# Large projections first, and the second half's norm inside the first half's projections

## The chip, the cores and the metric

The kernel runs on one core of a Trainium2 chip. The metric is the device time of one execution in microseconds, lower is better. A core has five engines with instruction queues of their own: TensorE (PE, with its weight loads shown as PEld), VectorE (DVE), ScalarE (ACT), GpSimd (POOL) and SyncE (SP), which here issues all DMA transfers of the program.

## What is computed

One step of a decoder trunk with two layers, for 1024 prompt tokens and 64 sample tokens (8 sequences of 8), with D = 1024. Layer 0 mixes with RWKV-7, layer 1 with sparse attention; both end with a feed-forward block. The change lies in layer 0, ahead of the recurrence:

```python
h = rms_norm(x, norm_g) * (1 + sc_a) + sh_a            # sh_a, sc_a, ... = SiLU(c) @ W_ada + b_ada
h_prev = concat([shift_prev, h[:, :-1]])
xr, xw, xk, xv, xa, xg = [h + (h_prev - h) * mix[n] for n in range(6)]
r, k, v = xr @ w_rkv[0], xk @ w_rkv[1], xv @ w_rkv[2]  # 1024 x 1024 each
w = tanh(xw @ w1) @ w2                                 # rank 64
a = sigmoid(a0 + (xa @ a1) @ a2)                       # rank 64
g = sigmoid(xg @ g1) @ g2                              # rank 160
S, y = wkv7_scan(S0, r, decay(w), k, v, a)             # over time, per head
out = (norm(y) + bonus) * g @ w_o
```

All six results are needed by the recurrence, g only at its end. They don't depend on each other.

## The kernel before

**Halves.** The 1088 tokens are worked on in two groups: GA holds the 64 sample tokens and prompt rows 0 to 511 (576 columns, in blocks of 320 and 256), GB the prompt rows 512 to 1023 (one block of 512). Activations lie transposed, features on partitions, as four tiles of [128, 2, 585] ("quarters"). The pool `xp` has four such tiles, enough for one group's x or h. `rwkv_h` writes h over x, and needs for GB the last column of GA's h (`lastA`).

**Projections.** `rwkv_proj(g, h)` is a generator. For each of the six inputs, `mixed` (L526) makes xn = h*(1-mix) + h_prev*mix in eight chunks and splits it into a rounded part and a remainder (hi, lo), and `mm3` (L133, matmuls in L140) multiplies in three terms: hi*wh, lo*wh, hi*wl. A large projection has 8 output blocks of 8 chunks; a low-rank one has a first matmul to the rank, an activation and a split, and a second one to 1024. Before, the three low-rank inputs (n = 1, 4, 5) come first and the three large ones (n = 0, 2, 3) after. All results go to a scratch tensor in DRAM (RA, RB; L591 and L600). The mixed inputs live in `act` (8 tiles, one set of hi and lo). During GA a second set, `act2`, and a pool `mx` for the temporaries exist, and the sets take turns; during GB there is one set.

**Conditioning.** `ada_steps` multiplies SiLU(c) with W_ada, 48 steps that each load 1 MB (L261) and take 16 matmuls (L264) and a fold (L250). Eight steps come before everything else. The other 40 are the generator `more`, stepped once at each of the 36 yields of GA's `rwkv_proj`; the rest runs behind it.

**Recurrence.** `wkv` runs 18 units of GA (16 prompt, 2 sample) and 16 of GB through four stages (prep, inv1, inv2, rec) that are interleaved. Its constants (L181, c_gmask and others) and tiles come from pools opened after those of the conditioning are closed, in the same memory. Each unit reads its columns of RA or RB (L672, and g in L813) and stores its result (YA or YB, L960). `projB()` is handed to `wkv` as `self.side`. The rate for GA's units is 0, so nothing of it is put between them by hand; at t == len(A), ahead of the stages of the last three GA units and of the first GB unit, the loop `for _ in self.side: pass` emits all of it. After that `first(GA)`, the output projection and feed-forward of GA, becomes the side work.

**Order.** A list scheduler turns the program into one fixed order per engine: where an instruction's inputs and tile slots are free, it may go ahead of earlier ones that are not ready, and of several that are ready the earlier one in the program goes first. So what stands later in the program fills idle time, as far as its tiles are free. On the chip each engine, SP too, takes its instructions in that order and waits where a semaphore isn't set yet.

Of the kernel before, what the change touches and what calls it, by code (L numbers as in the profile page):

```python
# [47 lines left out]
GA = Grp("A", 64, 0, 512)  # L48
GB = Grp("B", 0, 512, 512)
# [28 lines left out]
class Kern:  # L78
# [202 lines left out]
    def xtile(self, name, pool=None):  # L281
        return [(pool or self.xp).tile([128, 2, 585], F32, name=name, tag="x") for _ in range(4)]

    def load_x(self, g):
        nc = self.nc
        x = self.xtile("x")
        for c0, n, kind, r0 in g.tiles:
            src = self.I["x_sample"].rearrange("b t d -> (b t) d") if kind == "s" else self.I["x_prompt"][0, r0:r0 + 128]
            for hf in range(2):
                t = self.tmp("xin")  # L290
                nc.sync.dma_start(t[0:n, 0:512], src[:, hf * 512:hf * 512 + 512])
                o = self.mmt()
                for k in range(4):
                    nc.tensor.transpose(o[:, k * 128:k * 128 + n], t[0:n, k * 128:k * 128 + 128], self.ident[0:n, 0:n])
                ov = o.rearrange("p (q a b) -> p q a b", q=2, a=2)
                for q in range(2):
                    (nc.scalar.copy if q else nc.vector.tensor_copy)(x[hf * 2 + q][:, :, c0:c0 + n], ov[:, q, :, 0:n])
        return x
# [253 lines left out]
    def rwkv_proj(self, g, h):  # L552
        nc, W, I = self.nc, g.W, self.I
        R = self.rscr(g)
        self.kn[g.name] = self.cp.tile([128, len(g.tiles), 16], F32, name="kn" + g.name)

        for n, w1, w2, rk, slot in ((1, "rw_w1", "rw_w2", 64, 2), (4, "rw_a1", "rw_a2", 64, 3), (5, "rw_g1", "rw_g2", 160, 5)):
            xs = self.mixed(g, h, n)
            parts = [(0, min(rk, 128))] + ([(128, rk - 128)] if rk > 128 else [])
            mids = []  # L560
            for f0, fn in parts:
                hw, lw = self.loadw(I[w1][0, :, f0:f0 + fn].rearrange("(k p) f -> p k f", p=128), 128, 8 * fn)
                t = self.tmp("lt")

                def evac(o, c0, c1):
                    if n == 4:
                        nc.scalar.copy(t[0:fn, c0:c1], o[0:fn, 0:c1 - c0])
                    else:
                        nc.scalar.activation(out=t[0:fn, c0:c1], in_=o[0:fn, 0:c1 - c0], func=AF.Tanh, scale=(1.0 if n == 1 else 0.5))
                self.mm3(g, [(hw[:, k * fn:k * fn + fn], lw[:, k * fn:k * fn + fn]) for k in range(8)], xs, evac, M=fn)  # L570
                if n == 5:
                    nc.vector.tensor_scalar(out=t[0:fn, 0:W], in0=t[0:fn, 0:W], scalar1=0.5, scalar2=0.5, op0=ALU.mult, op1=ALU.add)
                a, b = self.tmp("lh", F32R), self.tmp("ll", F32R)
                self.split(t[0:fn, 0:W], a[0:fn, 0:W], b[0:fn, 0:W])
                mids.append((a[0:fn, 0:W], b[0:fn, 0:W]))
            ws = [self.loadw(I[w2][0, f0:f0 + fn, :], fn, 1024) for f0, fn in parts]
            for m in range(8):
                t = self.tmp("pt")

                def evac(o, c0, c1):  # L580
                    if n == 5:
                        nc.scalar.copy(t[:, c0:c1], o[:, 0:c1 - c0])
                    else:
                        i0 = (0 if n == 1 else 8) + m
                        nc.scalar.activation(out=t[:, c0:c1], in_=o[:, 0:c1 - c0], func=AF.Tanh, scale=0.5, bias=self.w0h[:, i0:i0 + 1])
                if m % 2:
                    yield
                self.mm3(g, [(hw[0:fn, m * 128:m * 128 + 128], lw[0:fn, m * 128:m * 128 + 128]) for (hw, lw), (_, fn) in zip(ws, parts)], mids, evac)
                if n != 5:
                    nc.vector.tensor_scalar(out=t[:, 0:W], in0=t[:, 0:W], scalar1=0.5, scalar2=0.5, op0=ALU.mult, op1=ALU.add)  # L590
                nc.sync.dma_start(R[m, :, slot, 0:W], t[:, 0:W])  # L591
        for n, i, slot in ((0, 0, 0), (2, 1, 1), (3, 2, 4)):
            xs = self.mixed(g, h, n)
            for m in range(8):
                yield
                hw, lw = self.loadw(I["rw_w_rkv"][0, i, :, m * 128:m * 128 + 128].rearrange("(k p) f -> p k f", p=128), 128, 1024)
                t = self.tmp("pt")
                self.mm3(g, [(hw[:, k * 128:k * 128 + 128], lw[:, k * 128:k * 128 + 128]) for k in range(8)], xs,
                         lambda o, c0, c1: nc.scalar.copy(t[:, c0:c1], o[:, 0:c1 - c0]))
                nc.sync.dma_start(R[m, :, slot, 0:W], t[:, 0:W])  # L600
                if i == 1:

                    if m == 0:
                        ss = self.kn[g.name]
                        if g.ns:
                            nc.vector.memset(ss[:, 0], 1.0)
                    sq = self.tmp("ks")
                    nc.scalar.activation(out=sq[:, 0:W], in_=t[:, 0:W], func=AF.Square, scale=self.rv["kk"][:, m:m + 1])
                    o = self.mmt()
                    for it, (c0, n_, _, _) in enumerate(g.tiles):  # L610
                        nc.tensor.matmul(o[0:n_, it * 2:it * 2 + 2], sq[:, c0:c0 + n_], self.hsel, start=True, stop=True)
                    nt = len(g.tiles)
                    for i0, i1, P in ((0, 1, 64), (1, nt, 128)) if g.ns else ((0, nt, 128),):
                        nc.vector.tensor_scalar(out=ss[0:P, i0:i1, m * 2:m * 2 + 2], in0=o[0:P, i0 * 2:i1 * 2].rearrange("p (i h) -> p i h", h=2),
                                                scalar1=1e-24, scalar2=None, op0=ALU.max)
                    if m == 7:
                        sv = ss.rearrange("p i h -> p (i h)")
                        y = self.rsqrt(None, sv, 128, nt * 16, "kn")
                        nc.vector.tensor_copy(sv, y)
# [934 lines left out]
            nc.sync.dma_start(self.scr["OA"][:, :, 0:64].rearrange("k p t -> p k t"), oTs)  # L1554

    def run(self):
        self.mark("setup" )
        self.setup()
        self.mark("ada_prep" )
# [23 lines left out]
        with ExitStack() as ctx:  # L1583
# [5 lines left out]
            more = more()  # L1589
            act, self.act2 = self.act, P("act2", 8)  # L1590
            self.mx = P("mx", 6)
            for _ in self.rwkv_proj(GA, hA):
                next(more, None)
            self.act = act
            self.act2 = self.mx = None
            for _ in more:
# [13 lines left out]
                pass  # L1610

        def projB():
            self.mark("load_xB")
            x = self.load_x(GB)
            self.mark("spill_xB")
            self.spill_x(GB, x)
            self.mark("rwkv_hB")
            h = self.rwkv_h(GB, x)
            self.mark("rwkv_projB")
            yield from self.rwkv_proj(GB, h)  # L1620

# [130 lines left out]
```

## Time and profile before

| | us |
|---|---|
| median of 3 runs | 4313.54 (4303.31 to 4316.45) |
| the profiled execution | 4326.98 |
| its span | 4325.0 |

The profile shows one execution. The page gives busy time per engine and, in 40 slices of the span, the TensorE clock that the chip granted in tenths of full speed (PEclk). The views used below are the table of windows (busy time of each engine in chosen stretches, with the granted clock and the DMA share), the groups of instructions by source line, the waits, and the timeline. In a group's row, "x400 | 27.8, 391" means 400 instructions, 27.8 us busy in all, 391 ns each, then the idle time of the engine before them and what ended it. Matmuls overlap in the pipeline, so the mean duration of one is longer than the distance from one to the next; where a count of matmuls is priced, busy time in a stretch divided by the count is used.

### The profile page before, as it was taken

The page shows a single profiled execution, that of the slowest core. Times are in us where ns is not written, and L with a number is a line of the kernel's source. Part 1 is how long each engine was busy: PE and PEld are TensorE (multiplying, and loading weights), DVE is VectorE, ACT ScalarE, POOL GpSimd, SP SyncE. Part 2 cuts the span into 40 slices and gives each one's busy share as a digit, 9 for nine tenths or more (in the row PEclk, how much of TensorE's full clock was granted, in tenths as well). Part 3 has the DMA queues.
Part 4 walks back from the last instruction along what each step waited for, and adds up shares of the span by engine and source line. Part 5 has one row for each costly group of instructions (what it writes and reads, how often), then busy time and mean ns, then how long its engine had stood idle before and what let it go on. Part 6 is the DMA issues. An engine that isn't in the chain of part 4 may idle for free. (4 is left out here: it accounts for less than half of the span.)

```text
span 4325.0 us, 77351 instructions
## 1 busy us (share of the span) xinstructions
PE 3993.6 (92%) x31120; PEld 3206.4 (74%) x31120; DVE 2521.2 (58%) x6174; ACT 1681.0 (39%) x3147; POOL 969.0 (22%) x762
## 2 busy tenths in 40 slices
PE   7998899989999999989799979988879999999999
PEld 4787665666777799989655656778666677998887
DVE  5512784533667655551886954452899855555444
ACT  5632564434445323331454323332443344333332
POOL 1321331312333222211111122222110000222322
PEclk6798697978899899989799989998888899999999
DMA  6676122314221122233332245444211112233332
GB/s 215 199 237 207 50 85 69 89 54 124 85 64 54 42 70 85 84 106 117 121 95 63 64 156 202 139 124 153 75 51 35 30 50 79 80 92 93 93 94 88
DMA packets 506743, 433.89 MB, mean 100 GB/s; under 512 B 93777, under 2 KB 451777, under 8 KB 501202
## 3 DMA queue, kind: packets, MB, share of 16 engines
q1 hardware_dynamic: 500498, 391.20, 29.9%
q0 software_dynamic: 5888, 37.75, 2.5%
q8 instruction: 245, 4.01, 0.4%
q14 instruction: 112, 0.92, 0.1%
HBM read 360.48 MB, written 67.87 MB: 99 GB/s over the span
## 5 line engine op out<-in xcount | busy, mean ns | idle before, releaser
L126 POOL TENSOR_TENSOR wl<-w,wh 128x1024 fp32r<-128x1024 f32 (+1 forms) x258 | 618.6, 2402 | 2326.5 <-ACT wh L122 2095.5
L140 PE MATMUL o<-hi,wh 128*128 128x512 f32 (+4 forms) x2592 | 884.1, 345 | 28.5 <-ACT hi L144 24.1
L140 PE MATMUL o<-lo,wh 128*128 128x512 f32 (+4 forms) x2592 | 885.9, 343 | 14.4 <-DVE lo L145 10.9
L140 PE MATMUL o<-hi,wl 128*128 128x512 f32 (+4 forms) x2592 | 881.7, 341 | 4.2 <-DVE wl L126 4.0
L122 ACT CAST wh<-w 128x1024 fp32r<-128x1024 f32 (+3 forms) x388 | 396.1, 1033 | 1010.6 <-PE o L140 829.9
L397 DVE SCALAR_TENSOR_TENSOR xr<-o,mods,xr 128x256 f32<-128x256 f32 (+1 forms) x816 | 463.0, 570 | 298.2 <-PE o L140 286.0
L140 PEld LDWEIGHTS o<-hi,wh 128*128 128x128 f32 (+1 forms) x2592 | 499.0, 194 | 80.7 <-ACT hi L144 28.0
L140 PE MATMUL o<-uh,wh 128*128 128x320 f32 (+2 forms) x1536 | 520.7, 339 | 39.8 <-DVE xr L397 31.8
L140 PEld LDWEIGHTS o<-lo,wh 128*128 128x128 f32 (+1 forms) x2592 | 499.6, 193 | 66.3 <-DVE lo L145 14.3
L140 PEld LDWEIGHTS o<-hi,wl 128*128 128x128 f32 (+1 forms) x2592 | 498.7, 193 | 53.7 <-issue 11.3
L140 PE MATMUL o<-uh,wl 128*128 128x320 f32 (+2 forms) x1536 | 514.2, 336 | 5.5 <-DVE tno L1220 3.7
L140 PE MATMUL o<-ul,wh 128*128 128x320 f32 (+2 forms) x1536 | 512.6, 334 | 0.0
L140 PEld LDWEIGHTS o<-uh,wh 128*128 128x128 f32 x1536 | 293.3, 191 | 77.9 <-DVE xr L397 37.5
L140 PEld LDWEIGHTS o<-uh,wl 128*128 128x128 f32 x1536 | 292.9, 191 | 33.6 <-issue 5.2
L126 DVE TENSOR_TENSOR wl<-w,wh 128x1024 fp32r<-128x1024 f32 (+2 forms) x130 | 184.9, 1423 | 223.3 <-ACT wh L122 222.9
L140 PEld LDWEIGHTS o<-ul,wh 128*128 128x128 f32 x1536 | 293.6, 191 | 25.5 <-issue 3.6
L145 DVE TENSOR_TENSOR ul<-z,uh 128x512 fp32r<-128x512 f32 (+1 forms) x128 | 124.7, 974 | 171.3 <-ACT uh L144 170.5
L1041 PE MATMUL o<-wl,hi 128*128 128x256 f32 (+2 forms) x648 | 189.6, 294 | 6.9 <-POOL wl L126 6.9
L1041 PE MATMUL o<-wh,hi 128*128 128x256 f32 (+2 forms) x648 | 188.7, 293 | 6.9 <-ACT hi L144 6.9
L1041 PE MATMUL o<-wh,lo 128*128 128x256 f32 (+2 forms) x648 | 185.0, 292 | 0.0
L1210 DVE TENSOR_SCALAR_CACHE_REDUCE tj<-sc,tcf 128x384 bf16<-128x384 f32 (+2 forms) x192 | 180.4, 939 | 2.4
L1282 ACT ACTIVATE sm<-sm,st 128x128 f32<-128x128 f32 (+7 forms) x128 | 99.3, 776 | 155.2 <-DVE st L1281 107.7
(415 smaller groups left out, 6902.0 us busy)
## 6 DMA issues: line engine op xcount, KB each, us to landing
w<-in_w_up SPq DMA_DIRECT2D x128, 512.0 KB
w<-in_w_down SPq DMA_DIRECT2D x128, 512.0 KB
wa<-in_w_ada SPq DMA_DIRECT2D x96, 512.0 KB
w<-in_rw_w_rkv SPq DMA_DIRECT2D x48, 512.0 KB
w<-in_att_w_in SPq DMA_DIRECT2D x32, 512.0 KB
RA<-pt SPq DMA_DIRECT2D x48, 288.0 KB
RB<-pt SPq DMA_DIRECT2D x48, 256.0 KB
in<-RA SPq DMA_DIRECT2D x32, 320.0 KB
```

Source lines behind the costliest of these rows:

```text
L122: nc.scalar.copy(h[:kp, :n], w[:kp, :n])
L126: eng.tensor_tensor(out=l[:kp, :n], in0=w[:kp, :n], in1=h[:kp, :n], op=ALU.subtract)
L140: nc.tensor.matmul(o[0:M, 0:c1 - c0], a, b[:, c0:c1], start=(i == 0 and q == 0), stop=(i == n - 1 and q == 2))
L145: (lo_eng or self.nc.vector).tensor_tensor(out=lo, in0=src, in1=hi, op=ALU.subtract)
L397: nc.vector.scalar_tensor_tensor(out=xm[:, p0:c1], in0=o[:, p0 - c0:c1 - c0], scalar=self.mods[l][:, j * 8 + m, 8:9], in1=xm[:, p0:c1], op ...
L1041: nc.tensor.matmul(o[0:n, 0:cw], a, w, start=(k == 0 and q == 0), stop=(k == 7 and q == 2))
L1210: nc.vector.tensor_scalar(out=junk[:, 0:L], in0=s, scalar1=th if isinstance(th, float) else th[:, i:i + 1], scalar2=None, op0=op, op1=ALU. ...
L1282: nc.scalar.activation(out=sm[:, 0:L], in_=sm[:, 0:L], func=AF.Exp, scale=-1.0, bias=mn[:, 0:1], accum_out=sums)
```

## The change

1. `rwkv_proj` is cut in two. The large projections become a generator `proj_rkv` of their own, which `rwkv_proj` runs first, for both halves; the low-rank ones follow.
2. GB's x is loaded, spilled and normed not at the start of `projB`, but inside GA's projections: when the ninth yield is reached (i == 8, at the first output block of the second large projection). Its four tiles come from a new pool `xpB` that is open during GA's projections. The resulting h is stored to a DRAM scratch `hB`.
3. `projB` loads h from `hB` into tiles of `xp` and goes straight to the projections.

The conditioning's generator is stepped as before, once at each of the 36 yields.

```diff
-    def load_x(self, g):
-        nc = self.nc
-        x = self.xtile("x")
+    def load_x(self, g, pool=None):
+        nc = self.nc
+        x = self.xtile("x", pool)
...
         self.kn[g.name] = self.cp.tile([128, len(g.tiles), 16], F32, name="kn" + g.name)
+        yield from self.proj_rkv(g, h)
 
         for n, w1, w2, rk, slot in ((1, "rw_w1", "rw_w2", 64, 2), (4, "rw_a1", "rw_a2", 64, 3), (5, "rw_g1", "rw_g2", 160, 5)):
...
                 nc.sync.dma_start(R[m, :, slot, 0:W], t[:, 0:W])
+
+    def proj_rkv(self, g, h):
+        nc, W, I = self.nc, g.W, self.I
+        R = self.rscr(g)
         for n, i, slot in ((0, 0, 0), (2, 1, 1), (3, 2, 4)):
...
             self.mx = P("mx", 6)
-            for _ in self.rwkv_proj(GA, hA):
+            xpB = P("xpB", 4)
+            for i, _ in enumerate(self.rwkv_proj(GA, hA)):
                 next(more, None)
+                if i == 8:
+
+                    xB = self.load_x(GB, xpB)
+                    self.spill_x(GB, xB)
+                    hB = self.rwkv_h(GB, xB)
+                    self.scratch("hB", [8, 128, 513])
+                    for q in range(4):
+                        nc.sync.dma_start(self.scr["hB"][q * 2:q * 2 + 2].rearrange("k p n -> p k n"), hB[q][:, :, 0:513])
...
         def projB():
-            self.mark("load_xB")
-            x = self.load_x(GB)
-            self.mark("spill_xB")
-            self.spill_x(GB, x)
-            self.mark("rwkv_hB")
-            h = self.rwkv_h(GB, x)
+            h = self.xtile("hr")
+            for q in range(4):
+                nc.sync.dma_start(h[q][:, :, 0:513], self.scr["hB"][q * 2:q * 2 + 2].rearrange("k p n -> p k n"))
             self.mark("rwkv_projB")
             yield from self.rwkv_proj(GB, h)
```

## The prediction

> **What bounds the kernel now.** I read the page first, for the engine that is full and for its clock.
>
> ```profile
> span 4325.0 us, 77351 instructions
> PE 3993.6 (92%) x31120; PEld 3206.4 (74%) x31120; DVE 2521.2 (58%) x6174; ACT 1681.0 (39%) x3147; POOL 969.0 (22%) x762
> PEclk6798697978899899989799989998888899999999
> ```
>
> PE is busy for 92% of the span, but in the first third its granted clock is low. So only two things can save time: stretches in which PE has no work, and stretches in which it works at half clock. The edited code runs in the first 1146 us, which I cut into stages with the table of windows (columns: stretch and length; busy time of PE, PEld, DVE, ACT, POOL; clock; DMA share; GB/s).
>
> ```profile
> 57.00:184.00 127.00, 114.67 (x606) 83.07 (x606) 77.59 (x128) 82.10 (x151) 40.25 (x23) 0.66 0.56 181
> 163.00:184.00 21.00, 21.00 (x88) 14.05 (x88) 4.01 (x9) 9.22 (x18) 5.18 (x3) 0.50 0.36 118
> 184.00:392.00 208.00, 206.12 (x1727) 186.10 (x1727) 45.54 (x96) 72.11 (x136) 49.91 (x25) 0.99 0.73 230
> 392.00:410.00 18.00, 13.30 (x105) 6.80 (x104) 3.25 (x11) 3.29 (x9) 0.74 (x1) 0.67 0.82 267
> 410.00:460.00 50.00, 32.45 (x285) 24.98 (x282) 37.23 (x98) 24.34 (x52) 14.27 (x26) 0.57 0.31 90
> 460.00:665.00 205.00, 190.27 (x2719) 133.39 (x2716) 158.28 (x462) 117.75 (x274) 73.23 (x101) 0.87 0.23 67
> 1040.00:1083.00 43.00, 42.83 (x202) 35.14 (x200) 12.56 (x20) 18.29 (x28) 13.13 (x7) 1.00 0.66 201
> ```
>
> 57 to 184 is the low-rank part of the first half (A), 184 to 392 its three large projections: PE full, clock 0.99. 392 to 410 are leftover steps of the conditioning (w_ada); 410 to 460 load and norm the second half (B) beside the first recurrence units, with PE at 32 of 50 us and clock 0.57. From 460 B's projections fill PE between the units of A. 1040 to 1083 is the other end of that filling, and four rows of SP's timeline show what it is.
>
> ```profile
> 644.50 0.37 SPq L960 DMA_DIRECT2D YA<-gt  x1
> 665.52 0.37 SPq L960 DMA_DIRECT2D YA<-gt  x1
> 1020.18 0.37 SPq L960 DMA_DIRECT2D YA<-gt  x1
> 1083.38 0.33 SPq L600 DMA_DIRECT2D RB<-pt  x1
> 1099.44 0.36 SPq L960 DMA_DIRECT2D YA<-gt  x1
> ```
>
> Each YA store ends a unit of A. Normally they are 21 us apart (644.50, 665.52); here 79 us pass. In program order all that is left of projB stands ahead of the last three A units (the loop that empties `self.side` at t == len(A)). PE does nothing else for 43 us, while the recurrence waits.
>
> ```profile
> 341.00:392.00 51.00, 45.61 (x340) 44.87 (x339) 1.00 0.62 195
> 460.00:1040.00 580.00, 217.59 (x584) 110.87 (x585) 0.82 0.25 71
> 1040.00:1083.00 43.00, 42.01 (x186) 34.39 (x184) 1.00 0.66 201
> ```
>
> These are the same windows for line 140 alone, the projection matmuls. At full clock one takes 45.61/340 = 0.134 us in A (two column blocks, 320 and 256) and 42.01/186 = 0.226 us in B (512 columns). The 43 us are a whole large projection: 8 x 24 x 0.226 = 43.4. B's 768 matmuls (576 large, 192 low-rank) would need 174 us; they take 217.6 + 42.0 = 260. So 86 us go to half clock and to matmuls stretched between others.
>
> **Part 1: large ahead of low-rank in A.** Rows of the groups, 184 to 392:
>
> ```profile
> L264 PE MATMUL oa<-wa,cst 128*32 128x256 f32 x400 | 27.8, 391 | 1.0 <-DMA wa<-in_w_ada 1.0
> L250 PE MATMUL pa<-fold,adas 128*128 128x10 f32 x95 | 14.5, 262 | 0.7 <-ACT adas L266 0.5
> L611 PE MATMUL o<-hsel,ks 128*128 128x2 f32 (+1 forms) x80 | 10.1, 244 | 0.2
> L539 DVE SCALAR_TENSOR_TENSOR xn<-x,vec,mt 128x512 f32<-128x512 f32 x13 | 13.0, 1000 | 0.0
> L537 DVE SCALAR_TENSOR_TENSOR xn<-x,vec,mt 128x64 f32<-128x64 f32 x13 | 5.9, 454 | 3.4 <-ACT mt L532 3.2
> L145 DVE TENSOR_TENSOR lo<-xn,hi 128x576 fp32r<-128x576 f32 x7 | 9.1, 1294 | 5.5 <-PE o L140 4.7 <-ACT hi L144 0.8
> 60.02 0.74 PE L140 MATMUL o<-hi,wh 128*64 128x320 f32 x2 [2.95 <-ACT hi L144]
> 182.39 0.41 PE L140 MATMUL o<-ll,wh 32*128 32x256 f32 x1
> ```
>
> The large part costs 24 x 48 x 0.134 = 154 us, 24 conditioning steps at (27.8 + 14.5)/25 = 1.7 us = 41, key norms 10: 205 of the 208 us seen. It is bound by PE and its order doesn't change that. The low-rank part needs 384 x 0.134 = 51 and 12 x 1.7 = 20, so 71 of its 127 us: the rest is the opening wait for `mixed` and half clock. One `mixed` is eight chunks of 1.0 + 0.45 + half of 1.29 = 2.1 us on DVE, 17 us. Some such wait stays at 60 us whichever projection is first: two of the eight output blocks (2 x 48 x 0.134 = 13 us) fit in it, so I charge 5. The low-rank inputs are then mixed under the third large projection (two sets of `act` tiles), which takes 17 off. Net -12, between -25 and +5. What I keep is the half clock: between 163 and 184 PE is busy for 21.00 of 21 us and still granted 0.50, on matmuls of which half, like the one at 182.39, use 32 rows.
> The Trainium skill, page "TensorE: Matmul & The Clock Gate", section "Part 1: The HAM clock gate", says the opposite: sustained matmuls open the gate within about 3.4 us and only an idle window closes it. The row above speaks against it; by the page the low-rank part would run near its full-clock time, which is the fourth rival below.
>
> **Part 2: B's load and norm inside A.** Groups between 385 and 460:
>
> ```profile
> L368 ACT ACTIVATE x<-hu,mods,gm 128x512 f32<-128x512 f32 x8 | 6.5, 810 | 3.0 <-DVE hu L359 3.0
> L294 PE MATMUL o<-c_ident,xin 128*128 128x128 f32 x32 | 5.7, 334 | 0.0
> L333 DVE TENSOR_TENSOR acc<-acc,sq 128x512 f32<-128x512 f32 x7 | 5.5, 786 | 0.9 <-ACT sq L331 0.8
> L359 DVE TENSOR_TENSOR hu<-x,rb 128x512 f32<-128x512 f32 x8 | 5.5, 682 | 1.5 <-ACT rb L352 1.5
> L297 DVE COPY x<-o 128x256 f32<-128x256 f32 x8 | 3.4, 426 | 2.5 <-PE o L294 2.4
> L351 PE MATMUL o<-c_ident,rsBy 128*128 128x128 f32 x8 | 1.9, 421 | 0.0
> L338 PE MATMUL o<-onec,acc 128*128 128x2 f32 x8 | 1.9, 356 | 1.7 <-DVE acc L333 1.7
> ```
>
> PE gets 5.7 + 1.9 + 1.9 = 9.5 us more in A. That can be 0 if the transposes slip into the opening, which needs only the new pool; 17 if PE, in order, also waits for the sums (a chain of adds and Newton steps). I take 9.5. DVE's 3.4 + 5.5 + 5.5 = 14.4 us lie under the large projections, where DVE is busy 46 of 208. Leaving 410 to 460, the same 14.4 no longer stand between the first units' instructions: -7, half of it, between -14 and 0.
> New on SP: four stores of hB and four loads, 0.53 MB each; 4.2 MB at 230 GB/s are 18 us of transfer, in stretches with a DMA share of 0.73 or less. The eight loads of x and four spills only move. A store of hB waits for L368, and behind it stand weight loads that PE needs; SP mostly waits anyway:
>
> ```profile
> SPq L261 <- PE oa L264: 106.3, 32, 7.1
> ```
>
> so I charge 0, at most 8. The loads of hB wait until A's last `mixed` has read hA; behind them on SP stand the last stores of A and the units' loads, which no engine needs before the conditioning ends. `first(GA)`'s reload of x waits in the same way for B's last `mixed`, as before.
>
> **Part 3: what the end of A releases.** The recurrence's constants are the first thing after the conditioning, in memory that its tiles held:
>
> ```profile
> 410.11 0.33 SPq L181 DMA_DIRECT2D c_gmask<-in_c_gmask  x1
> 457.74 0.73 ACT L532 ACTIVATE mt<-x,mix 128x513 f32<-128x513 f32 x1
> ```
>
> Five conditioning steps are left over after 36 yields; behind a PE that is full they can't start early, and from 392 they are paced by their loads. Behind the low-rank part, where PE is idle 12 of 127 us and at half clock, I expect most to slip in: -12, between -18 and 0.
> B's first `mixed` starts at 457.74 now. Afterwards it needs only hB and A's first `act` set, both free before A's last low-rank outputs, so B's large projections can fill PE from about 390. Supply: PE's idle time between 392 and 460 is 4.7 + 17.6 = 22 us, the 9.5 us are gone from there, and of the 86 us lost in B's matmuls dense early filling should recover some 12. Together 43.5, against the 43.4 that stand at 1040. What may remain is a piece of the last low-rank projection. The gap of 79 less 21 is 58 us; I take 45 of it, between 0 and 58.
>
> **Sum.** -12 + 9.5 - 7 - 12 - 45 = -66.5 us. Against the profiled execution (4326.98 us, span 4325.0) that is 4260.5. This execution lay 13.4 us above the median of the three runs, 4313.54, so in the runs I expect 4247.
>
> **Rivals.**
> 1. *The surplus is not usable*: no change. Units run at 21 us with DVE busy 158 of 205 us, so more filling on PE delays them as much as it advances B, a low-rank projection stands at 1040 instead of a large one, and the conditioning still ends last. Only part 2's 7 us are left: 4306. Against it: the idle 22 us.
> 2. *The low-rank work is exposed at both ends*: slower. In A nothing hides it (no -12, +5, B's PE work with its waits +17). At t == len(A) the last low-rank projection of B and half of another are open: in A the last one took 126 to 184, 58 us, so about 64 instead of 43. 5 + 17 + 21 = +43, 4357. It decides once more than one low-rank projection of B is open when unit 18 starts. For it: DVE's load in 460 to 665, which slows every `mixed`. Against it: B starts 70 us earlier.
> 3. *The norm doesn't move where it says*: nothing but the new pool holds back the loads of x, so they may run in the opening, beside the w_ada loads. 2 MB at 230 GB/s delay those by up to 9 us: 4256, within the forecast's own range.
> 4. *Full clock in the low-rank part*: 127 - 71 = 56 us are lost now, of which I have already taken 17; the other 39 would go too: 4208. Against it: the 163 to 184 row.
>
> **How the numbers follow.** Forecast (with rival 3) 0.66, rival 4 0.07, rival 1 0.14, rival 2 0.13. Its own range is 4210 to 4295 (parts 2 and 3 at their best give -102, 4212; with their savings halved and their costs at the upper ends, -19, 4295). Chances: a measurement of this kernel tells about 0.3%, 13 us, from no change. Faster by more: 0.66 + 0.07 + a quarter of rival 1 = 0.77; within: 0.10; slower: 0.13. For 8 in 10 the range runs from 4195, which takes in rival 4, to 4312, which takes in rival 1 and leaves out rival 2 and the outer ends.
>
> **What would show it.** Right: large stores (RA) from about 75 to 290 us and low-rank ones last; constants issued before 400; B's first `mixed` before 400; YA stores near 1020 without a gap of 79. Wrong in part 1: the low-rank part over 120 us, or under 90 (rival 4). Wrong in part 3: constants still after 405, or a pure block of B's matmuls of 30 us or more ahead of the last A units. The forecast fails as a whole if that block remains, for it carries 45 of the 66 us.

## The result and the profile after

The changed kernel is slower: 4351.16 us in the median of 20 runs (4337.28 to 4372.57), against 4314.99 for 20 runs of the kernel before. The ratio is 1.0106, with a 95% interval of 1.0083 to 1.0128. By the ratio 46 us are lost, by the medians 36, where 66.5 were to be gained. Runs of one kernel differ mostly by the mean clock that they were granted: the changed kernel took 4372.35 us at 0.910 and 4337.28 at 0.920. The loss is not such a difference, for at 0.917 the changed kernel took 4343.95 to 4350.04 us, and the kernel before 4311.09 and 4317.08 (two of its runs beside e13 to e16). The profiled execution took 4343.95 us at 0.917, the one of the kernel before 4326.98 at 0.911. The two traces thus lie only 17 us apart, where the medians lie 36 apart.

The page of the changed kernel, engine totals and clock (tenths of full speed, 40 slices):

```profile
span 4342.2 us, 77414 instructions
PE 3983.3 (92%) x31120; PEld 3190.3 (73%) x31120; DVE 2534.5 (58%) x6174; ACT 1683.1 (39%) x3147; POOL 964.9 (22%) x762
PEclk7896798888898999999799989998888899999999
```

The same number of matmuls keeps PE busy for about as long (3993.6 before). So PE's work hasn't grown; it stands in other places. The table of windows of the changed kernel, cut at its own stages (columns as in the prediction):

```profile
57.00:135.00 78.00, 71.61 (x552) 63.01 (x548) 48.40 (x64) 46.35 (x78) 34.34 (x17) 0.91 0.76 237
135.00:180.00 45.00, 24.91 (x180) 18.63 (x181) 24.27 (x68) 23.78 (x44) 5.28 (x4) 0.77 0.84 240
180.00:309.00 129.00, 127.62 (x1013) 119.74 (x1014) 30.28 (x66) 45.11 (x83) 29.92 (x15) 0.96 0.56 178
309.00:431.00 122.00, 114.27 (x616) 83.30 (x615) 39.18 (x65) 50.17 (x101) 19.21 (x12) 0.67 0.51 165
431.00:455.00 24.00, 15.14 (x100) 6.62 (x100) 1.34 (x8) 1.84 (x6) 0.00 (x0) 0.50 0.77 240
1017.00:1112.00 95.00, 78.03 (x358) 45.24 (x356) 58.43 (x109) 59.57 (x104) 16.83 (x14) 0.76 0.42 139
```

57 to 309 are now A's large projections: 252 us where they took 208. 309 to 431 are the low-rank ones, 122 for 127, still at clock 0.67. 431 to 455 is the conditioning's rest, 24 for 18, at half clock. The sum is 398 for 353: the recurrence's constants come 45 us later.

Most of the 44 us in the large part, some 35, stand in one row of that table, 135 to 180: the load and norm of B. (The other 9 are the opening, as e8 shows below.) SP's timeline brackets the row by the stores of two neighbouring output blocks of A; the two rows behind them show the distance of the next ones:

```profile
130.54 0.33 SPq L605 DMA_DIRECT2D RA<-pt  x1
175.51 0.49 SPq L605 DMA_DIRECT2D RA<-pt  x1
191.35 0.34 SPq L605 DMA_DIRECT2D RA<-pt  x1
201.29 0.34 SPq L605 DMA_DIRECT2D RA<-pt  x1
```

One output takes 45 us where the next ones take 16 and 10. What PE waited for between 130 and 180 (view of the waits: total us, times, longest) names the norm's own chain, link by link, and the conditioning held up beside it:

```profile
PE oa L264 <- DMA wa<-in_w_ada: 6.1, 4, 2.3
PE pa L250 <- ACT adas L266: 4.2, 1, 4.2
PE o L351 <- DVE rsBy L173: 3.5, 1, 3.5
PE o L294 <- ACT x L297: 2.8, 1, 2.8
PE o L338 <- DVE acc L333: 2.5, 1, 2.5
PE o L519 <- DVE lastB L508: 2.5, 1, 2.5
```

The second place is where B's projections start. SP's timeline around the constants; then ACT's row of A's last `mixed`, ACT's row of B's first one, and PE's first matmul of B; then the two largest of SP's own waits between 340 and 460:

```profile
454.75 0.35 SPq L181 DMA_DIRECT2D c_gmask<-in_c_gmask  x1
...
457.05 1.38 SPq L818 DMA_DIRECT2D gt<-RA  x3
458.47 2.04 SPq L1630 DMA_DIRECT2D hr<-hB  x4
```

```profile
347.91 0.79 ACT L532 ACTIVATE mt<-x,mix 128x585 f32<-128x585 f32 x1
462.25 0.72 ACT L532 ACTIVATE mt<-hr,mix 128x513 f32<-128x513 f32 x1 [2.10 <-DMA hr<-hB]
480.18 0.80 PE L140 MATMUL o<-hi,wh 128*128 128x512 f32 x1
```

```profile
SPq L261 <- PE oa L264: 33.6, 18, 6.1
SPq L592 <- ACT pt L583: 32.9, 8, 6.4
```

ACT begins its last reading of A's rows at 347.91 (DVE at 350.13), so their place is free soon after; hB has been in DRAM since about 170. Yet the four loads go out at 458.47, behind all loads of the conditioning and behind the constants, in a queue that spent 66 us of that stretch waiting for the conditioning's matmuls and for A's last outputs. B's first `mixed` waits for them. It comes at 462.25, not before 400 as forecast, and 4.5 us later than before the change. PE's first matmul of B comes at 480.18; before the change it came at 462.07.

The third place is the other end. The last stores of A's units and of B's outputs, changed kernel:

```profile
1003.22 0.37 SPq L965 DMA_DIRECT2D YA<-gt  x1
...
1016.81 0.32 SPq L605 DMA_DIRECT2D RB<-pt  x1
1035.82 9.06 SPq L592 DMA_DIRECT2D RB<-pt  x8
1061.06 8.04 SPq L592 DMA_DIRECT2D RB<-pt  x8
1094.16 14.63 SPq L592 DMA_DIRECT2D RB<-pt  x7
1111.63 0.32 SPq L592 DMA_DIRECT2D RB<-pt  x1
1117.84 0.37 SPq L965 DMA_DIRECT2D YA<-gt  x1
```

The gap between the 15th and 16th YA store was 79 us and is 115: all three low-rank projections of B (L592) stand in it, 95 us in the window 1017 to 1112. In between the units ran faster: from the first YA store (505.46 before, 541.42 after) to the 15th it took 515 us and takes 462. So the lead of the kernel before is 45 us at the constants, 36 at the first YA store, -17 at the 15th, 18 at the 16th and 24 at the last one (1145.01 and 1169.02).

### The profile page after: what moved, and what is told of

Its sections match the earlier page's. It is cut to its first block, busy times and chain, and to the rows that moved or that the text cites. A ratio compares the mean times of both kernels' runs of the same rounds, so it can differ in the third digit from the quotient of the medians.

```text
span 4342.2 us, 77414 instructions
## 1 busy us (share of the span) xinstructions
PE 3983.3 (92%) x31120; PEld 3190.3 (73%) x31120; DVE 2534.5 (58%) x6174; ACT 1683.1 (39%) x3147; POOL 964.9 (22%) x762
## 5 line engine op out<-in xcount | busy, mean ns | idle before, releaser
L126 POOL TENSOR_TENSOR wl<-w,wh 128x1024 fp32r<-128x1024 f32 (+2 forms) x258 | 618.8, 2403 | 2320.1 <-ACT wh L122 2155.5
L140 PE MATMUL o<-hi,wh 128*128 128x512 f32 (+3 forms) x2592 | 887.8, 346 | 24.9 <-ACT hi L144 20.5
L140 PE MATMUL o<-lo,wh 128*128 128x512 f32 (+3 forms) x2592 | 886.6, 343 | 12.7 <-DVE lo L145 11.4
L140 PE MATMUL o<-hi,wl 128*128 128x512 f32 (+3 forms) x2592 | 881.7, 341 | 1.9 <-DVE tno L1225 0.9
L122 ACT CAST wh<-w 128x1024 fp32r<-128x1024 f32 (+2 forms) x388 | 396.0, 1033 | 962.7 <-PE o L140 791.5
L126 DVE TENSOR_TENSOR wl<-w,wh 128x1024 fp32r<-128x1024 f32 (+3 forms) x130 | 183.8, 1414 | 214.7 <-ACT wh L122 214.1
```

The lines of the kernel that those rows point to most:

```text
L122: nc.scalar.copy(h[:kp, :n], w[:kp, :n])
L126: eng.tensor_tensor(out=l[:kp, :n], in0=w[:kp, :n], in1=h[:kp, :n], op=ALU.subtract)
L140: nc.tensor.matmul(o[0:M, 0:c1 - c0], a, b[:, c0:c1], start=(i == 0 and q == 0), stop=(i == n - 1 and q == 2))
```

## The experiments

Each kernel was timed beside the kernel before, in five rounds, 6 to 12 runs of each. Kernels that were not timed side by side are compared by their ratios to it; 0.01 of a ratio is 43 us. "The barrier" is the point where all that is left of B's projections stands ahead of A's last three units. In the expectations, N, O, T1 to T5, A and W are names of theories, explained where they first stand.

Three parts were changed: A's order, B's order, and the place of B's norm. The kernel before, the changed one and six of the runs are their eight combinations. The table shows the ratio to before, the times of the constants' load, of the first and 15th YA store and of the last one, the gap behind the 15th, and how many of B's 48 output blocks were stored ahead of the 15th.

```
kernel   A's order   B's order   B's norm  ratio [95% interval]      const   1st YA  15th YA  gap    last YA  outputs
before   low-rank    low-rank    in projB  1                         410.11  505.46  1020.18   79.3  1145.01  38
e8       large       low-rank    in projB  1.0028 [1.0004, 1.0052]   420.02  505.53  1015.94   83.6  1159.62  37
e7       low-rank    large       in projB  0.9997 [0.9972, 1.0021]   412.44  502.95   987.54  117.0  1154.72  20
e1       large       large       in projB  1.0073 [1.0043, 1.0103]   420.20  510.56  1005.68  119.0  1174.86  20
e2       low-rank    low-rank    in A      0.9963 [0.9934, 0.9992]   439.06  529.75  1028.49   54.8  1125.89  41
e3       large       low-rank    in A      1.0028 [0.9998, 1.0058]   455.82  540.45  1025.77   60.8  1130.50  40
e9       low-rank    large       in A      0.9900 [0.9866, 0.9933]   434.50  517.00  1004.52   70.8  1117.21  32
changed  large       large       in A      1.0106 [1.0083, 1.0128]   454.75  541.42  1003.22  114.6  1169.02  21
```

**First round: the block in A, or the barrier?** The trace left two theories. T1: the loss is the 45 us block of the norm. T2: it is the three low-rank projections at the barrier.

e1: the order alone.

```diff
-                if i == 8:
-                    xB = self.load_x(GB, xpB)
...
         def projB():
-            h = self.xtile("hr")
+            x = self.load_x(GB)
+            self.spill_x(GB, x)
+            h = self.rwkv_h(GB, x)
```

> The order alone: large projections first in both halves, the second half loaded and normed behind the first half's projections, as before the change. Theory T1 (the 45 us by which the recurrence's constants come later are the load and norm of the second half, which stand in TensorE's order ahead of the second large projection: 45 us for one output block in place of some 9): without them the constants are issued at 410 to 425 us (410.11 before, 454.75 after), and the kernel takes about as long as before, 4305 to 4330. Rival T2 (the loss is at the barrier, where three low-rank projections of the second half, 95 us, stand in place of one large one, 43 us): the constants come early as well, but the YA stores keep a gap of 110 to 120 us ahead of the last two, and the time is 4340 or more.

Constants at 420.20, as T1 said, but 4343.17 us and a gap of 119.0, as T2 said.

e2: the norm alone. `yield from self.proj_rkv(g, h)` goes back behind the low-rank loop, and the norm to the first block of the second large projection.

```diff
-                if i == 8:
+                if i == 20:
```

> The norm alone: low-rank projections first in both halves as before, the second half loaded, normed and stored behind the first output block of the second large projection, the same place in the work as in the changed kernel. T1: the output block beside the norm takes 40 to 50 us again, the constants come at 440 to 455, and the time is 4335 to 4355. T2: the gap of the YA stores falls to 45 to 80 us, and the time is 4315 or less, late constants or not.

4300.09 us, faster than before (0.9963), although the constants come at 439.06: the block is there as in the changed kernel, and pays for itself. T1 as the whole cause falls.

e3: the changed kernel with B's order undone.

```diff
-        yield from self.proj_rkv(g, h)
+        if g.ns:
+            yield from self.proj_rkv(g, h)
...
+        if not g.ns:
+            yield from self.proj_rkv(g, h)
```

> As the changed kernel, but the second half does its low-rank projections first, as before the change; the first half is as in the changed kernel. T1: the constants stay at 450 to 460 and the time at 4335 to 4355, since what is done late at the barrier is only what was not done earlier. T2: the gap of the YA stores falls from 115 to 45 to 80 us and the time by 25 to 45, to 4305 to 4325.

4316.70 us, gap 60.8: as T2 said. 0.78 points of ratio come back.

e4: the changed kernel with the norm behind A's projections in the program.

```diff
-                if i == 8:
-                    xB = self.load_x(GB, xpB)
...
+            xB = self.load_x(GB, xpB)
+            self.spill_x(GB, xB)
+            hB = self.rwkv_h(GB, xB)
```

> As the changed kernel, but the second half's load, norm and stores come behind all projections of the first half in the program, ahead of the rest of the conditioning. T1: large outputs run without the 45 us block, the constants come at 410 to 425 if the norm runs beside the conditioning's rest, at 440 to 460 if it runs ahead of it; the time follows them, 4315 to 4330 or 4345 to 4360. T2: the gap of the YA stores stays at 105 to 120 and the time within 10 us of the changed kernel's 4351, wherever the norm runs.

Constants at 445.55, 4334.72 us (1.0042, from 1.0015 to 1.0068), a gap of 114.8. The constants are where T1 has 4345 to 4360 and the gap where T2 has 4341 to 4361; the time is below both.

**Second round: each part alone.** If T2 were the cause, turning round B's order alone should cost what the order costs.

e5 and e6: the norm alone once more, beside the third low-rank projection of A (`i == 9` in place of 20), and behind all of A's projections.

> Low-rank projections first in both halves, and the second half's load and norm in the low-rank part of the first half (beside the third low-rank projection, where TensorE is granted half clock) in place of beside the second large one. Theory N (beside a large projection the norm costs TensorE some 30 us of waiting, because its chain stands in TensorE's order; the low-rank part waits anyway): the constants come at 415 to 430 us (439.06 with the norm beside the large one, 410.11 before), the gap of the YA stores stays at 50 to 70, and the time is 4270 to 4292. Rival O (the chain costs its waits wherever it stands): the constants at 435 to 450 and the time at 4295 to 4310.

> Low-rank projections first in both halves, and the second half's load, norm and stores behind all projections of the first half in the program, ahead of the conditioning's rest. With large projections first this place put the constants at 445.55, 25 us later than without any norm there. N: the chain stands alone there, beside nothing but the conditioning's rest, so the constants come at 425 to 440 and the time is 4295 to 4315. O: the same constants; the two differ in the run with the norm in the low-rank part.

Constants at 433.20 and 429.04, 4304.25 us (0.9968) and 4297.99 (0.994, from 0.9909 to 0.9971). Theory N expected less than 4292 and constants by 430 for the first: missed. Rival O's time is met, its constants (from 435) just aren't. By time the three places can't be told apart; wherever it stands in one piece beside A's old order, the norm puts the constants 19 to 29 us later.

e7 and e8: only B's order, and only A's order, by the `if g.ns` of e3 or its opposite, with the norm in projB.

> Only the second half's projections are turned round (large first); the first half and the place of the norm are as before the change. Theory T2 (the three low-rank projections of the second half stand alone at the barrier, 95 us, where one large one took 43): constants at 408 to 413, the gap of the YA stores 110 to 120, the time 4328 to 4345. Rival T3 (what made the order alone slower is the first half's order, whose constants came 10 us later): the time within 10 us of before, 4306 to 4326.

> Only the first half's projections are turned round (large first); the second half and the place of the norm are as before the change. The prediction's part 1 gave 12 us less for this and 12 less for the conditioning's rest: constants at 385 to 400, the time 4290 to 4305. T2: the constants at 415 to 425 as in the run of the order alone, the gap of the YA stores at 70 to 85 as before, the time 4315 to 4330. T3: the time 4335 or more.

e7: 4317.52 us, 0.9997. The gap grew to 117.0 as T2 said, and it cost nothing: the units ahead of it ran from 502.95 to 987.54, 30 us faster than before. T2 as told falls as well: a long gap is no loss if its time was gained ahead of it. e8: 4328.15 us, 1.0028, constants at 420.02 where the prediction's parts 1 and 3 together made some 386. All three of T2's marks for e8 are met; T3, which e7's time had met, wanted 4335 or more. The table of windows of e8 shows why:

```profile
57.00:274.00 217.00, 209.82 (x1687) 190.15 (x1688) 90.51 (x150) 100.74 (x178) 69.98 (x35) 0.96 0.67 211
274.00:397.00 123.00, 115.60 (x623) 85.03 (x621) 39.66 (x65) 50.43 (x102) 19.22 (x12) 0.67 0.51 164
397.00:420.00 23.00, 14.43 (x97) 5.92 (x96) 1.12 (x6) 1.49 (x4) 0.00 (x0) 0.50 0.81 250
```

The large part takes 217 us for 208, now that the opening wait lies in it. The low-rank part gets 4 us shorter, not 17. The conditioning's rest is 23 us, not less than 18.

**Third round: the last combination, and the block.** T4: large first in B can't use an early norm.

e9: norm in A and B's order, A's order as before.

> The norm of the second half at the first block of the second large projection, as in the norm alone, and the second half's projections turned round (large first); the first half keeps its low-rank projections first. With the norm behind, turning round the second half cost nothing (ratio 0.9997). Theory T4 (large first, the filling takes the same matmuls and so leaves all three low-rank projections for the barrier, however early it starts; the time the early norm frees cannot be turned into a shorter gap): the gap of the YA stores 110 to 120, the time 4320 to 4342, so 20 to 40 above the norm alone (4300). Rival A (the two parts add up: norm alone and the second half's order alone): the time 4293 to 4308.

4281.68 us, ratio 0.99, from six runs: the fastest of the eight, and T4 falls. It is below rival A's range too, so the two parts gain more than their sum. Beside A's old order, B's large-first order with the early norm gains 1.0%; beside A's new order the same two parts lose. A's order costs 0.28 points alone and 2.06 between this kernel and the changed one.

e10: the norm alone (as e2), its chain dealt out: one link at each output block of the second large projection, the sums and the spread root held in two buffers of their own.

```diff
-                if i == 20:
-                    xB = self.load_x(GB, xpB)
-                    hB = self.rwkv_h(GB, xB)
...
+                if i >= 20:
+                    next(dealt, None)
```

> As the norm alone, but the load and norm of the second half are dealt out over the output blocks of the second large projection: load at one block, squares and sums at the next, row sums and root, spreading and scaling, last rows, each at a block of its own, with two buffers for what is held between them. Theory N2 (the block's cost is TensorE waiting in program order for the norm's chain): each of its matmuls then finds its inputs ready, the constants come at 415 to 425 us in place of 439.06, and the time is 4272 to 4290. Rival W (the cost is the work and its transfers, shared slots or queues, not the order): constants at 432 to 442 and the time 4293 to 4306.

Constants at 418.02, 4282.55 us (0.9897, from 0.9861 to 0.9934). PE's waits between 248 and 290 in e2 (first fence) and between 248 and 300 in e10 (second), all rows of over half a us:

```profile
PE pa L250 <- ACT adas L266: 4.3, 2, 3.8
PE o L351 <- DVE rsBy L173: 2.5, 1, 2.5
PE o L338 <- DVE acc L333: 2.2, 1, 2.2
PE o L519 <- DVE lastB L508: 1.7, 1, 1.7
PE oa L264 <- DMA wa<-in_w_ada: 1.3, 3, 0.8
PE o L294 <- ACT x L297: 1.0, 2, 0.8
```

```profile
PE o L294 <- ACT x L297: 1.4, 2, 0.8
PE pa L250 <- ACT adas L266: 0.6, 1, 0.6
```

The waits for the chain are gone, and with them 21 us up to the constants. The block was order on PE, as theory N2 had it, and W falls.

e11: e10 with five conditioning steps more in the low-rank part (a second `next(more, None)` at five yields).

> As the norm dealt out, and five of the conditioning's steps that are left over behind the projections are taken at five yields of the low-rank part. If the 18 us tail (392 to 410 before) is those steps paced by their loads, the constants come 10 to 20 us before those of the norm dealt out and the time is 5 to 20 lower; if the loads themselves end last (DMA share 0.82 in the tail), the constants come at most 5 us earlier and the time stays within 8.

A miss: 4302.37 us, constants at 426.33. The rest behind the projections is gone, the constants follow the last large output at once; but the low-rank part grew by 21 us, 149 where e10 has 128 (PE busy 129.60 and 114.78). Five steps cost more there, at clock 0.65, than their 18 us at the end.

e12: the changed kernel with the norm dealt out, from `i >= 8`.

> The changed kernel with both orders as it has them, but the second half's norm dealt out over the output blocks of the second large projection. N2: constants at 420 to 432 in place of 454.75, the gap of the YA stores still 110 to 120, and the time 4315 to 4335 in place of 4351: the block is some 20 to 30 us of the change's loss, the rest is the order. W: constants at 445 to 456 and the time 4340 to 4356.

Constants at 432.51, 22 us earlier, but 4342.60 us (1.0045, from 1.0016 to 1.0074), above N2's range and in W's, and a gap of 116.6. By the ratios 0.61 points of the loss come back (0.24 to 0.98). It has e9's constants and e9's unit times up to the 15th YA store (1000.73 and 1004.52), but 21 outputs of B stored by then, where e9 has 32. So late constants aren't the main part of what lies between e9 and the changed kernel.

**Fourth round: the start of B.** What differs is when B's projections begin. Timeline rows of e9, SP and ACT:

```profile
304.49 0.43 SPq L1633 DMA_DIRECT2D hr<-hB  x1
...
333.23 1.04 SPq L1633 DMA_DIRECT2D hr<-hB  x1
```

```profile
412.53 1.96 ACT L532 ACTIVATE mt<-hr,mix 128x513 f32<-128x513 f32 x3
```

There the loads go out under A's last large projection, and B's inputs are mixed 50 us earlier than in the changed kernel. In e9's program they stand behind the constants as well; why the scheduler moved them ahead here and not there no run shows. What it makes of the two stretches 380 to 455 and 455 to 541 shows in the windows of e9 (first fence) and the changed kernel (second):

```profile
380.00:455.00 75.00, 70.86 (x516) 58.16 (x515) 25.26 (x49) 29.32 (x53) 21.59 (x20) 0.99 0.60 186
455.00:541.00 86.00, 84.17 (x1225) 59.68 (x1225) 55.85 (x166) 42.66 (x103) 37.64 (x49) 0.97 0.29 83
```

```profile
380.00:455.00 75.00, 66.10 (x371) 40.85 (x363) 4.64 (x17) 14.43 (x35) 3.12 (x2) 0.62 0.59 186
455.00:541.00 86.00, 66.33 (x862) 46.42 (x862) 67.97 (x153) 42.87 (x94) 36.07 (x49) 0.84 0.39 118
```

PE does 508 matmuls more in the same 161 us, at nearly full clock. That the late start makes this difference is theory T5.

e13: the changed kernel, only hB's loads earlier.

```diff
+                if i == 32:
+                    self.hr = self.xtile("hr")
+                    for q in range(4):
+                        nc.sync.dma_start(self.hr[q][:, :, 0:513], self.scr["hB"][q * 2:q * 2 + 2].rearrange("k p n -> p k n"))
...
         def projB():
-            h = self.xtile("hr")
-            for q in range(4):
-                nc.sync.dma_start(h[q][:, :, 0:513], self.scr["hB"][q * 2:q * 2 + 2].rearrange("k p n -> p k n"))
+            h = self.hr
```

> The changed kernel with both orders and the norm as it has them; only the loads of hB are issued from within the first half's last low-rank projection, in place of behind the conditioning's loads and the recurrence's constants (458.47 us). Theory T5 (the loss is that the second half's projections start only then: loads at 458, first mixed inputs at 462, where with the first half's low-rank projections ahead they were loaded at 304 to 333 and mixed from 412): first mixed inputs before 440, at least 25 of 48 outputs of the second half stored ahead of the 15th YA store (21 in the changed kernel, 32 in the run of norm and second half's order), the gap of the YA stores at most 105, and the time 4310 to 4335. Rival A (the first half's order costs by its constants, 20 us later, and by half clock at the low-rank end, not by the start): outputs 21 to 23, gap 110 to 120, time 4340 to 4355.

4309.16 us, ratio 0.9972 (0.9952 to 0.9993), against 1.0106: an edit that moves four loads in the program, and nothing else, turns the loss into a small gain. (The scheduler then orders what follows anew.) In medians it is 42 us, by the ratios 58 (45 to 71). Rows of e13, SP's, ACT's and PE's first matmul of B:

```profile
384.61 2.14 SPq L1612 DMA_DIRECT2D hr<-hB  x4
457.76 13.29 SPq L120 DMA_DIRECT2D w<-in_rw_w_rkv  x5
```

```profile
422.97 0.73 ACT L532 ACTIVATE mt<-hr,mix 128x513 f32<-128x513 f32 x1
463.81 0.79 PE L140 MATMUL o<-hi,wh 128*128 128x512 f32 x1
```

T5's start is met, and its time is missed by less than 1 us, towards faster. Two of its marks aren't met: 22 outputs are stored by the 15th YA store, and the gap is 107.2. The gain came as faster units, whose 15th store stands at 986.11 in place of 1003.22. The mixing moved by 39 us, PE's first matmul of B only by 16: B's weights (L120) are other loads, and they still go out behind the constants.

One reservation on the size: e13's runs were granted mean clocks of 0.918 to 0.925, those of the changed kernel 0.910 to 0.920. The two profiled executions, at 0.918 and 0.917, lie 21 us apart. What raised the clock in e13's other runs no trace shows.

e14: e9 with hB's stores behind the conditioning's rest in the program, to start B later.

> The run of norm and second half's order (4281.68), with the early start taken away: the four stores of hB come behind the conditioning's rest in the program, so that their loads, and with them the second half's first mixed inputs, come some 30 us or more later. T5: fewer than 29 outputs ahead of the 15th YA store (32 there), a gap of 85 to 115 in place of 71, and the time 4300 to 4325. Rival A: outputs 30 to 32, the gap within 10 of 71, and the time 4275 to 4292.

4306.65 us (0.9954, from 0.9926 to 0.9983), in T5's range, but its first `mixed` came at 420.20, 8 us later and not 30, and 32 outputs and a gap of 73.3 are rival A's. It doesn't decide between the two.

e17: e9 with A's rows held until the conditioning has ended, so that hB can't be loaded into their place before.

```diff
         self.ada_fin(1, 1)
+        hold = self.cp.tile([128, 4], F32, name="hold")
+        for q in range(4):
+            nc.vector.tensor_tensor(out=hold[:, q:q + 1], in0=hA[q][:, 0, 0:1], in1=self.mods[1][:, 47, 8:9], op=ALU.add)
```

> The run of norm and second half's order (4281.68), with the first half's rows held until the conditioning has ended: four additions of one column each read them together with the conditioning's last result, so that hB can be loaded into their place only then, behind the constants as in the changed kernel. Everything else is as in that run, the first half's order (low-rank first) too. T5 (the start of the second half's projections carries the loss): first mixed inputs at 440 to 470 in place of 412.53, TensorE busy for 64 to 74 of the 86 us from 455 to 541 (84.17 there, 66.33 in the changed kernel), the last YA store at 1135 to 1155 in place of 1117.21, and the time 4305 to 4330. Rival A (the first half's order costs by its own length and half clock): TensorE busy for 80 or more, and the time 4275 to 4292.

4311.25 us, ratio 0.9995 (0.9971 to 1.002), against 0.99. In medians 30 us, by the ratios 41 (23 to 59). Rows of e17: SP and ACT, then the two windows.

```profile
440.73 1.97 SPq L1636 DMA_DIRECT2D hr<-hB  x4
```

```profile
444.38 1.34 ACT L532 ACTIVATE mt<-hr,mix 128x513 f32<-128x513 f32 x2 [0.51 <-DMA hr<-hB]
```

```profile
380.00:455.00 75.00, 60.00 (x449) 50.44 (x447) 16.14 (x40) 19.99 (x40) 20.42 (x19) 0.82 0.57 179
455.00:541.00 86.00, 83.61 (x1217) 59.06 (x1217) 63.26 (x176) 47.11 (x109) 37.85 (x49) 1.00 0.29 81
```

The last YA store (1148.13) and the time are as T5 said. PE's share of 455 to 541 isn't: what is missing lies earlier, 60.00 for 70.86 of 75 us, at clock 0.82 for 0.99. And the outputs fall from 32 to 22, with a gap of 101.0: with a later start the filling ends at the same place as in the changed kernel, large ones done, low-rank ones open.

e15 and e16: the versions that the runs point to. e15 is e9 with the norm dealt out, e16 is e13 with the norm dealt out.

> The run of norm and second half's order with the norm dealt out over the output blocks of the second large projection. The constants come at 412 to 420 in place of 434.50 and, if the two gains add up (dealing out brought 18 us with the other order), the time is 4255 to 4272; if the filling is bound by TensorE from there on, 4272 to 4285.

> The changed kernel with the norm dealt out (4342.60) and the early loads of hB together. T5: first mixed inputs before 420, at least 25 outputs ahead of the 15th YA store, a gap of at most 105, the time 4300 to 4325. Rival A: 21 to 23 outputs, 110 to 120, the time 4332 to 4350.

e15: 4262.52 us, ratio 0.9862 (0.9829 to 0.9896), the fastest kernel of all, 1.4% under before, as if the two gains added up. Its constants come at 426.47, later than expected. e16: 4290.40 us (0.9931, from 0.9904 to 0.9959); it keeps both of the change's orders and is faster than before. Its time is below T5's range, its first `mixed` stands at 406.01, and its outputs (22) and gap (107.3) stay as in e13, short of T5's marks. Against e12 it shows once more what the loads' place is worth with the norm dealt out: 52 us in medians, 49 by the ratios (32 to 66).

## Why the prediction was wrong, step by step

**Part 3, B starts "from about 390": the step that failed.** The forecast counted on hB and the `act` set being free, and on the loads of hB having only stores and unit loads "behind them on SP". It was the other way round: the loads stood behind everything that the conditioning still had to load, and behind the constants (458.47). Asking when their inputs and their place were free gives about 350; asking what is ahead of them in the queue gives 458. Of the 72 us from 390 to 462.25, 39 are this place (e13: 422.97); the other 33 go with A's projections, which end at 431 and not at 392, by parts 1 and 2 below. Brought forward, the loads give 42 to 58 us (e13) or 49 to 52 (e16 against e12); held back in the fast combination (e17) they cost 30 to 41. Of the 70 us (by the ratios 89) between e9 and the changed kernel, the start is thus about half, with the reservation made at e13.

What the other half is stays open. Three things go with A's order. The constants come 20 us later than e9's, and dealing out the norm, which takes 22 us off them, brings 0.61 points back (e12). The low-rank end leaves half clock to what follows. And the first load of B's weights goes out behind the constants, at 460.55 (e13: 457.76), where in e9 it goes out at 390.22: PE's first matmul of B stands at 480.18, in e13 at 463.81, in e9 at 417.04. No run moves the weights alone. e16, with constants and first `mixed` about where e9 has them, is 0.31 points above e9 (from -0.12 to 0.74), no longer clearly apart.

The Trainium skill, page "DMA: Bandwidth & Descriptors", section "Anatomy of one DMA — SWDGE (gpsimd) path", says that a wait on a semaphore is spent on the sequencer that issues, ahead of dispatch. SP's rows agree: its queue waited 33.6 us for the conditioning's matmuls and 32.9 us for A's outputs, and hB's loads went out right behind the constants, over 100 us after their place was read for the last time.

**Part 3, the barrier at -45.** The gap grew by 35 us. "A piece of the last low-rank projection" was to remain, three whole ones did. But the forecast's measure was wrong too: e7 has the same long gap and loses nothing. The end of A's units is what counts, not the gap.

**Part 3, the conditioning's rest at -12.** It became 24 us for 18. The steps didn't slip into the low-rank part: 80 matmuls of L264, five steps, stand behind the projections, where before 64 stood. Where e11 forced five steps into the low-rank part (in A's old order), they cost more.

**Part 1 at -12.** A's order alone is 0.28% slower, and puts the constants 10 us later. The opening costs 9 (5 were charged). The 17 us for mixing under the third large projection could not be had: the prediction's own row, PE busy for 114.67 of 127 us, leaves 12 us of idle time in the whole part. The rest above the 71 us of full-clock time is time in which PE was busy, at a mean clock of 0.66. That the half clock stays was right, 115.60 busy of 123 at 0.67, and rival 4 fell with it.

**Part 2 at +9.5, at most 17.** The block holds some 35 us. That bound counted the waits for the sums alone; each link of the chain waits (the six rows of waits above), and the output's own matmuls stand behind the last one. Dealt out, the constants come 8 to 22 us earlier (e15, e10, e16, e12). The charge of nothing for hB's stores on SP fits e10, which has them too and whose constants come 8 us later than before, no more than the 9.5 of PE's work; the loads are the step above. That the norm's departure from 410 to 460 is worth something was right: e2 gains 0.37% although its constants come 29 us later.

**Rival 2 came nearest**, with 4357 predicted and 4351 measured, and its condition came true (more than one low-rank projection open). But its terms came out otherwise: opening 9 for 5, norm 35 for 17, gap 35 for 21, and units that ran 53 us faster, which it didn't have. It charged the gap as a loss, which e7 speaks against, and it doesn't name the late start. So the nearness of its number is in part luck. What the prediction held against it, "B starts 70 us earlier", is the very step that failed.

## What to carry to other kernels

When a change lets a transfer start earlier, ask for its place in the issuing queue and what waits ahead of it there, not only for its inputs and its buffer; and ask the same for the other loads that the work needs, here B's weights. Work put under other work in one piece makes TensorE wait at each link of its chain; dealt out over its neighbours it cost 21 us less here. And changes that each look neutral or good can lose together: three parts of 0.28, -0.03 and -0.37% gave 1.06%, and two of them without the third gave -1.00%.

## What the runs showed of the hardware

The half clock goes with the low-rank part, wherever it stands: it was granted 0.66 ahead of the large projections (PE busy for 114.67 of 127 us) and 0.67 behind them (114.27 of 122). What comes next is touched as well: the conditioning's rest ran at 0.50 behind low-rank projections (431 to 455) and at 0.67 behind large ones (392 to 410). PE is idle for part of both rests, so the runs don't show whether that or what ran ahead of them sets their clock. Inside the low-rank part, idle time isn't needed: between 400 and 420 in the changed kernel PE is busy for 20.00 of 20 us and granted 0.50, like in the prediction's row 163 to 184. What sets it there no run shows. Five conditioning steps put into the low-rank part (e11) added 15 us of PE time, 3 us each, where the prediction's rows give 1.7 for one in the large part.
